# Mean of x squared on 16 columns instead of 512, its norm spread through DRAM on SyncE's queue, and two constant rows loaded through GpSimd's queue

## The chip, the cores and the metric

One core of a Trainium2 chip runs the whole program. The metric is the device time of one execution in microseconds (us); lower is better. TensorE (PE in the profile) multiplies matrices, VectorE (DVE), ScalarE (ACT) and GpSimd (POOL) work on tiles of 128 partitions, and SyncE (SP) issues most of the transfers between memory (DRAM) and the on-chip tiles. ACT and POOL can issue transfers too; each of the three has its own queue, and all of them are carried out by the core's 16 DMA engines.

## The reference

One block of a streaming encoder on 512 positions of 1024 channels. What the change touches is its first step, the root-mean-square norm of the input x and the product of the normed x with `w_in`, and the layer norm of v in the spatial gating unit, with its scale g_v and offset b_v:

```python
def rms_norm(x, g):
    xf = x.astype(jnp.float32)
    y = xf * lax.rsqrt(jnp.mean(xf * xf, axis=-1, keepdims=True) + EPS)
    return (y * g.astype(jnp.float32)).astype(x.dtype)

    hn = rms_norm(h, g_mix_pre[i])
    proj = hn @ w_in[i]
    z_sgu, z_conv, z_pool, z_gate = jnp.split(proj, SPLITS, axis=-1)

def spatial_gating(z, w_s, b_s, g_v, b_v):
    u, v = jnp.split(z, 2, axis=-1)
    v = layer_norm(v, g_v, b_v)
    ...
```

Behind this stand a convolution branch, a pooling branch, three gates, a SwiGLU layer and a gated embedding, which the change leaves as they are.

## The kernel before, in words

Activations lie with channels on partitions: a tile of 128 channels x 512 positions, eight tiles (`KT`) for the 1024 channels. Every operand of a product is split into a high and a low part (`hi`, `lo`, type fp32r), and a product is three matmuls per tile of 128 channels: hi x hi, hi x lo and lo x hi (`mm3`). PE therefore runs through one long row of matmuls of 128x512, each with 128x128 weights.

The start of the program is arranged so that PE need not wait for the norm of x. `first_product` multiplies x, scaled by `g_mix_pre` but not yet normed (tiles `xg`, split by `x_high` on ACT and `x_low` on DVE), with six blocks of weights (`first`, `first_raw`), 18 matmuls for each of the eight channel tiles k, into the six banks `ps_first`. The norm is multiplied in afterwards, when `glu` reads these banks (`sig<-ps_first,x_inv`). While those matmuls run, DVE and ACT work out the norm: the squares of the eight x tiles are added into `x_sums` (128x512), `split_sums` splits that into two halves, two matmuls with a 128x128 matrix of 1/1024 (`channel_mean`) give the mean, the same in all 128 partitions, and `rsqrt`, eight DVE operations of 128x512, gives `x_inv`, 1/rms for every position on every partition. Then eight tiles `hn` are made: DVE multiplies x by gain and `x_inv` (`nrm`), ACT rounds that to the high part, DVE subtracts for the low part. All products behind `ps_first` read `hn`, the first of them `ps_ag`.

The later two norms of the kernel (`h_inv` and `conv_inv`) go another way, which this change uses for x too. `part_sums` transposes the 128x512 sums in blocks of 32x32 and adds along the free axis, which leaves four partial sums per position in a tile of 128x16 (`parts`, split in `part_halves`). `part_mean` adds those with two matmuls of 128x32 weights (`quarters`) on 16 columns. `rsqrt` then runs on 32x16 (`few`). `spread` transposes the result, writes it as one row of 512 numbers to DRAM (`row_home`) and reads that row back into all 128 partitions.

Weights come through `Weights`: SP loads a raw block (128x1024, three buffers), and it is split into `hi` and `lo` (three buffers each) a fixed number of blocks ahead of its product. For the blocks of the first stage from channel tile 5 on, and for the first two blocks `raw` behind them, the split is `split_dma`: ACT writes the high part and its negative, and a transfer on POOL's queue adds the raw block to it in memory (`accum_op`). From then on the split is one cast on ACT and one subtraction on DVE. The `hi` and `lo` of channel tile 7 of the first stage lie in buffers of that same ring, so the third block (`raw`, `hi`, `lo` of `ps_ag`'s third product) can be split only after PE has read them for the last time.

The rows g_v and b_v of the layer norm of v are loaded as two broadcasts of 128x1024 (`g_bc`, `b_bc`) into buffers that the first stage's weights give back; they are used from some 140 us on.

The order of the work is that of the code inside `with order()`; elsewhere a scheduler places it. The part from `x_square` to `hn` is in such a block as far as DVE's and ACT's own instructions go; a split of a weight block, and what `glu` does, are placed among them by the scheduler. An engine works its instructions off in a fixed order, and a transfer is issued when the engine that issues it has got to it and what it waits for has come.

Of the kernel before, what the change touches and what calls it, by code (L numbers as in the profile page):

```python
# [15 lines left out]
P = 128  # L16
T = 512
H = 256
D = 1024
KT = D // P  # L20
NB = T // P
Q = 32
# [71 lines left out]
def hybrid_block(  # L94
# [7 lines left out]
    nc = tc.nc  # L102
# [20 lines left out]
    def slot(tag, name, dt=F32R, shape=(2, T)):  # L123
        return act.tile([P, *shape], dt, tag=tag, name=name, bufs=6 if tag == "tm" else 8)

    def t2(name, n=T):
        return tmp.tile([P, n], F32, tag="t2", name=name)

    def row(name):
        return stat.tile([P, T], F32, tag="row", name=name)  # L130
# [7 lines left out]
    def first_cuts(k):  # L138
        return ((0, 2 * P), (2 * P, N_FIRST)) if k == 0 else ((0, N_FIRST),)
# [14 lines left out]
    def col(name, k):  # L154
        i = VECS.index(name) * KT + k
        return vec[:, i:i + 1]
# [16 lines left out]
    few = [const.tile([Q, Q], F32, name=f"few{i}") for i in range(3)]  # L173
# [15 lines left out]
    def split(hi, lo, src):  # L189
        act_e.copy(hi, src)  # L190
        dve.tensor_tensor(out=lo, in0=src, in1=hi, op=ALU.subtract)
# [52 lines left out]
    def blk(w, k):  # L244
        return w[:, k * P:(k + 1) * P]
# [33 lines left out]
    def rsqrt(y, a, t):  # L279

        dve.tensor_scalar(out=y.bitcast(I32), in0=a.bitcast(I32), scalar1=-0.5,
                          scalar2=RSQRT_SEED, op0=ALU.mult, op1=ALU.add)
        dve.tensor_tensor(out=t, in0=y, in1=y, op=ALU.mult)
        dve.scalar_tensor_tensor(out=t, in0=t, scalar=-RSQRT_C2 * RSQRT_S, in1=a,
                                 op0=ALU.mult, op1=ALU.mult)
        dve.scalar_tensor_tensor(out=y, in0=t, scalar=RSQRT_C1 * RSQRT_S, in1=y,
                                 op0=ALU.add, op1=ALU.mult)
        third_order(y, a, t)
# [12 lines left out]
    def third_order(y, a, t):  # L301

        dve.tensor_tensor(out=t, in0=y, in1=y, op=ALU.mult)
        dve.tensor_tensor(out=t, in0=t, in1=a, op=ALU.mult)
        dve.scalar_tensor_tensor(out=t, in0=t, scalar=-10.0 / 3.0 * RSQRT_S ** 2, in1=t,
                                 op0=ALU.add, op1=ALU.mult)
        dve.scalar_tensor_tensor(out=y, in0=t, scalar=5.0 * RSQRT_S ** 4, in1=y,
                                 op0=ALU.add, op1=ALU.mult)

    def channel_mean(sums, halves=None):  # L310


        ps = psum.tile([P, T], F32, tag="pst", name="ps_stat", bufs=1)
        ps = ps[:, :sums.shape[1]]
        if halves is None:
            pe.matmul(ps, lhsT=mean_mat.bitcast(F32), rhs=sums, start=True, stop=True)
        else:
            for i, half in enumerate(halves):
                pe.matmul(ps, lhsT=mean_mat, rhs=half, start=i == 0, stop=i == 1)
        return ps  # L320

    def part_sums(sums):

        turned, parts = t2("turned"), t2("parts", T // Q)
        dve.transpose(out=turned, in_=sums)
        dve.tensor_reduce(out=parts, in_=turned.rearrange("p (c q) -> p c q", q=Q),
                          axis=mybir.AxisListType.X, op=ALU.add)
        dve.tensor_copy(part_halves[:, 0], parts)
        dve.tensor_tensor(out=part_halves[:, 1], in0=parts, in1=part_halves[:, 0], op=ALU.subtract)

    def part_mean():

        ps = psum.tile([P, T], F32, tag="pst", name="ps_stat", bufs=1)[:Q, :T // Q]
        for i in range(2):
            pe.matmul(ps, lhsT=quarters, rhs=part_halves[:, i], start=i == 0, stop=i == 1)
        return ps

    def spread(y, few, turned):

        dve.transpose(out=turned, in_=few)  # L340
        home = dram.tile([1, T], F32, name="row_home")
        nc.scalar.dma_start(out=home.rearrange("o (c a) -> (o c) a", a=Q), in_=turned[:T // Q])
        nc.scalar.dma_start(out=y, in_=home.broadcast_to([P, T]))

    def spread_inv_rms(y):
        inv, t, turned = few
        rsqrt(inv[:, :T // Q], part_mean(), t[:, :T // Q])
        spread(y, inv, turned)

    def split_sums(sums):  # L350
        halves = [tmp.tile([P, T], F32R, tag="t2", name="sum_half") for _ in range(2)]
        split(*halves, sums)
        return halves
# [87 lines left out]
    x_sums = row("x_sums")  # L441
# [8 lines left out]
    def x_high(k):  # L450
        act_e.activation(out=xg[k][:, 0], in_=x_all[:, k], func=AF.Copy, scale=col("g_mix_pre", k))

    def x_low(k):
        dve.scalar_tensor_tensor(out=xg[k][:, 1], in0=x_all[:, k], scalar=col("g_mix_pre", k),
                                 in1=xg[k][:, 0], op0=ALU.mult, op1=ALU.subtract)

    def w_split(k):
        for c0, c1 in first_cuts(k):
            hi, lo = (w[:, c0:c1] for w in first[k])
            (split_dma if k >= DMA_K else split)(hi, lo, first_raw[k][:, c0:c1])  # L460

    def x_square(k):
        add_square(x_sums, x_all[:, k], k, dve)
# [45 lines left out]
    x_inv = row("x_inv")  # L509
# [3 lines left out]
    def first_product(k, passes, js=range(2 * N_RAW)):  # L513
        for w, a in passes:
            for j in js:
                pe.matmul(banks[j], lhsT=blk(first[k][w], j), rhs=xg[k][:, a],
                          start=k == 0 and w == a == 0, stop=k == KT - 1 and w == 1)


    passes = ((0, 0), (0, 1), (1, 0))  # L520
    with order():
        (c0, c1), cut = first_cuts(0)
        hi, lo = (w[:, c0:c1] for w in first[0])
        dve.tensor_copy(hi, first_raw[0][:, c0:c1])
        x_high(0)
        dve.tensor_tensor(out=lo, in0=first_raw[0][:, c0:c1], in1=hi, op=ALU.subtract)
        x_low(0)
        hi, lo = (w[:, slice(*cut)] for w in first[0])
        split(hi, lo, first_raw[0][:, slice(*cut)])
        first_product(0, passes, range(c1 // P))  # L530
        first_product(0, passes, range(c1 // P, 2 * N_RAW))
        x_square(0)
        x_high(1)
        w_split(1)
        x_low(1)
        x_square(1)
        x_square(2)
        first_product(1, passes)
        x_high(2)
        w_split(2)  # L540
        x_low(2)
        for k in range(3, 6):
            x_square(k)
        first_product(2, passes)
        x_high(3)
        w_split(3)
        for k in range(6, KT):
            x_square(k)
        x_low(3)
        for k in (4, 5):  # L550
            x_high(k)
            w_split(k)
            if k == 4:
                x_halves = split_sums(x_sums)
            x_low(k)
        first_product(3, passes[:2])
        ps_x = channel_mean(x_sums, x_halves)
        first_product(3, passes[2:])
        for k in range(4, KT):
            if k >= 6:  # L560
                x_high(k)
                w_split(k)
        weights.ahead(2)
        weights.split = split
        rsqrt(x_inv, ps_x, t2("rs_t"))
        x_low(6)
        x_low(7)
        low = None
        for i in range(KT):
            t = t2("nrm")  # L570
            dve.scalar_tensor_tensor(out=t, in0=x_all[:, i], scalar=col("g_mix_pre", i),
                                     in1=x_inv, op0=ALU.mult, op1=ALU.mult)
            act_e.copy(hn[i][:, 0], t)
            if low:
                low()
            low = lambda i=i, t=t: dve.tensor_tensor(out=hn[i][:, 1], in0=t, in1=hn[i][:, 0],
                                                     op=ALU.subtract)
        low()
        for k in range(4, KT):
            first_product(k, passes)  # L580
# [59 lines left out]
        dve.bn_stats(out=v_stats[:, b, c, :], in_=v)  # L640

    g_bc = slot("tm", "g_bc", F32, (D,))
    nc.sync.dma_start(out=g_bc, in_=gb_v[0:1, :].broadcast_to([P, D]))
    b_bc = slot("tm", "b_bc", F32, (D,))
    nc.sync.dma_start(out=b_bc, in_=gb_v[1:2, :].broadcast_to([P, D]))
    for _ in natural(v_all, v_gelu, TAPS[1]):
        pass
    mv = const.tile([P, NB, 2], F32, name="v_mv")
# [186 lines left out]
    for k in range(KT):  # L835
        ln_center(k)
    part_sums(var_sum)
    spread_inv_rms(conv_inv)
    for k in range(KT):
        ln_out(k)  # L840
# [74 lines left out]
    with order():  # L915
# [18 lines left out]
        for i in range(N_HALF):  # L934
            n = KT - N_HALF + i
            mean = (lambda: inv_rms(o_sums[:, lo_half], o_inv[:, lo_half],
                                    rsqrt=table_rsqrt)) if i == 0 else None
# [36 lines left out]
        def norm_h(done):  # L974
            if done == STAT_H:
                spread_inv_rms(h_inv)
# [191 lines left out]
```

## Time and profile before

| what | number |
|---|---|
| median of 3 runs | 968.01 us (967.85 to 968.63) |
| the profiled execution's own time | 967.84 us |
| its span | 965.9 us |
| PE busy | 960.6 us, 99% of the span, 4331 matmuls |
| DVE busy | 659.8 us, 68% |
| ACT busy | 354.4 us, 37% |
| POOL busy | 72.1 us, 7% |
| granted clock of PE | 1.0 |

The span is from the first to the last instruction of the profiled execution. Rows of the timeline give the start in us, the duration in us, the engine, the line, the operation, and output <- inputs with shapes; `xN` means that N instructions were merged into the row. All of the work of helper functions carries line 81, so operations are told apart by their tiles. What an engine waited for stands in brackets at the end of a row. `ACTq`, `SPq` mean the issue of a transfer by that engine.

### The profile page before, as it was taken

What the parts mean: (1) busy time and instruction counts of PE and PEld (TensorE: products, weight loads), DVE (VectorE), ACT (ScalarE), POOL (GpSimd) and SP (SyncE); (2) the same over time, 40 slices, a digit from 0 to 9 for tenths busy, and PEclk for the clock granted to TensorE, in tenths of its full rate; (3) what the DMA queues carried; (4) which work ended last, traced back from release to release, by engine and by line L of the source; (5) the groups of instructions that cost most, each with busy time, mean ns of one, the idle gap of its engine ahead of it and who ended that gap; (6) DMA issues with size and microseconds to landing.
All of it is one profiled execution on the core that took longest, in us unless ns stands there. A gap on an engine that the chain in (4) does not pass through costs nothing.

```text
span 965.9 us, 11032 instructions
## 1 busy us (share of the span) xinstructions
PE 960.6 (99%) x4331; PEld 797.1 (83%) x4331; DVE 659.8 (68%) x870; ACT 354.4 (37%) x471; POOL 72.1 (7%) x55
## 2 busy tenths in 40 slices
PE   9999999999999999999999999999999999999998
PEld 6888888888888888888888988888888888888886
DVE  7987899999997799985655786544454432223583
ACT  7622323343124432247435444333232322223451
POOL 1100014001013602220000000000000000000000
PEclk9999999999999999999999999999999999999999
DMA  8832332563323233232336313232323233334321
GB/s 299 196 106 89 110 107 66 172 170 117 108 87 99 86 103 106 88 113 95 109 125 211 101 44 98 89 108 88 110 88 100 94 86 100 96 101 143 111 76 56
DMA packets 36837, 107.45 MB, mean 111 GB/s; under 512 B 4273, under 2 KB 8881, under 8 KB 36785
## 3 DMA queue, kind: packets, MB, share of 16 engines
q1 hardware_dynamic: 35568, 103.95, 33.2%
q0 software_dynamic: 720, 2.23, 1.3%
q10 hardware_dynamic: 496, 0.57, 0.2%
q8 instruction: 34, 0.56, 0.2%
q14 instruction: 19, 0.15, 0.0%
HBM read 100.30 MB, written 4.20 MB: 108 GB/s over the span
## 4 chain that ended last, share of the span: by engine, by line
PE 99%; DVE 0%; issue 0%; DVEq 0%
PE ps_f L81 25%; PE ps_gate L81 14%; PE ps_br L81 14%; PE ps_fo L81 12%; PE ps_nat L81 9%; PE ps_ag L81 6%; PE ps_o L81 5%; PE ps_z L81 5%; PE ps_pg L81 5%; PE ps_first L81 3%; PE ps_pool L81 1%; PE ps_ple L81 1%; PE ps_mix L81 1%; PE ps_warm L81 0%; PE ps_stat L81 0%; DVE pg L81 0%
## 5 line engine op out<-in xcount | busy, mean ns | idle before, releaser
L81 ACT CAST hi<-raw 128x1024 fp32r<-128x1024 f32 (+2 forms) x161 | 165.9, 1032 | 441.2 <-PE ps_br L81 83.9
L81 DVE TENSOR_TENSOR lo<-raw,hi 128x1024 fp32r<-128x1024 f32 (+2 forms) x159 | 210.2, 1323 | 108.5 <-ACT hi L81 108.2
L81 PE MATMUL ps_f<-hg,hi 128*128 128x512 f32 (+1 forms) x604 | 183.4, 385 | 0.0
L81 DVE SCALAR_TENSOR_TENSOR acc<-h_conv,vec,acc 128x511 f32<-128x511 f32 (+17 forms) x240 | 177.1, 742 | 4.5
L81 PEld LDWEIGHTS ps_f<-hg,hi 128*128 128x128 f32 x604 | 112.6, 188 | 22.8
L81 PE MATMUL ps_gate<-hn,hi 128*128 128x512 f32 x384 | 118.7, 389 | 0.0
L81 PE MATMUL ps_f<-hg,lo 128*128 128x512 f32 (+1 forms) x302 | 114.4, 385 | 0.0
L81 PE MATMUL ps_fo<-f,hi 128*128 128x512 f32 x352 | 108.4, 389 | 0.0
L81 PEld LDWEIGHTS ps_gate<-hn,hi 128*128 128x128 f32 x384 | 72.1, 188 | 15.0
L81 PE MATMUL ps_nat<-hi,hn 128*128 128x512 f32 x256 | 78.7, 389 | 0.0
L81 PEld LDWEIGHTS ps_fo<-f,hi 128*128 128x128 f32 x352 | 66.1, 188 | 13.7
L81 PE MATMUL ps_gate<-hn,lo 128*128 128x512 f32 x192 | 74.7, 389 | 0.0
L81 PE MATMUL ps_fo<-f,lo 128*128 128x512 f32 x176 | 68.5, 389 | 0.0
L81 PEld LDWEIGHTS ps_f<-hg,lo 128*128 128x128 f32 x302 | 56.3, 188 | 11.2
L81 PEld LDWEIGHTS ps_nat<-hi,hn 128*128 128x128 f32 x256 | 48.0, 188 | 9.9
L81 DVE TENSOR_TENSOR f<-ps_f,h_inv 128x512 f32<-128x512 f32 x22 | 15.2, 689 | 56.5 <-PE ps_f L81 56.5
L81 PE MATMUL ps_nat<-lo,hn 128*128 128x512 f32 x128 | 49.8, 389 | 0.0
L81 PE MATMUL ps_ag<-hn,hi 128*128 128x512 f32 x160 | 49.2, 389 | 0.0
L81 DVE TENSOR_TENSOR silu<-ps_f,h_inv 128x512 f32<-128x512 f32 x22 | 15.2, 690 | 43.7 <-PE ps_f L81 35.9
L81 PEld LDWEIGHTS ps_gate<-hn,lo 128*128 128x128 f32 x192 | 36.0, 188 | 7.4
L81 PE MATMUL ps_br<-pool,hi 128*128 128x512 f32 x128 | 39.7, 389 | 0.0
L81 PE MATMUL ps_z<-hn,hi 128*128 128x512 f32 x128 | 39.7, 389 | 0.0
(229 smaller groups left out, 1450.0 us busy)
## 6 DMA issues: line engine op xcount, KB each, us to landing
raw<-in_w_mix SPq DMA_DIRECT2D x90, 512.0 KB, 3.3
raw<-in_w_ffn_in SPq DMA_DIRECT2D x44, 512.0 KB, 3.3
raw<-in_w_ffn_out SPq DMA_DIRECT2D x16, 448.0 KB, 3.3
raw<-in_w_ffn_out SPq DMA_DIRECT2D x8, 512.0 KB, 3.5
raw<-in_w_ple_gate SPq DMA_DIRECT2D x8, 512.0 KB, 3.8
x_all<-in_xT SPq DMA_DIRECT2D x8, 256.0 KB, 6.6
home<-corners SPq DMA_DIRECT2D x32, 64.0 KB, 2.6
sgu<-home SPq DMA_DIRECT2D x8, 256.0 KB, 2.7
```

Source lines behind the costliest of these rows:

```text
L81: inst = op(*args, **kw)
```

## The change

Three things are done.

- The mean of x squared is made the narrow way: `part_sums` on DVE in place of `split_sums` (ACT and DVE), `part_mean` in place of `channel_mean`, after all 18 matmuls of channel tile 3 instead of after 12 of them, and `rsqrt` on 32x16.
- The result is spread through DRAM to `x_inv`, by two transfers that wait for one another. `spread` gets a parameter for the queue; for x it is SP's, for the other two norms it stays ACT's.
- `g_bc` and `b_bc` are loaded through POOL's queue.

```diff
-    def spread(y, few, turned):
+    def spread(y, few, turned, queue=nc.scalar):
 
         dve.transpose(out=turned, in_=few)
         home = dram.tile([1, T], F32, name="row_home")
-        nc.scalar.dma_start(out=home.rearrange("o (c a) -> (o c) a", a=Q), in_=turned[:T // Q])
-        nc.scalar.dma_start(out=y, in_=home.broadcast_to([P, T]))
-
-    def spread_inv_rms(y):
+        queue.dma_start(out=home.rearrange("o (c a) -> (o c) a", a=Q), in_=turned[:T // Q])
+        queue.dma_start(out=y, in_=home.broadcast_to([P, T]))
+
+    def spread_inv_rms(y, queue=nc.scalar):
         inv, t, turned = few
         rsqrt(inv[:, :T // Q], part_mean(), t[:, :T // Q])
-        spread(y, inv, turned)
+        spread(y, inv, turned, queue)
...
             if k == 4:
-                x_halves = split_sums(x_sums)
+                part_sums(x_sums)
             x_low(k)
-        first_product(3, passes[:2])
-        ps_x = channel_mean(x_sums, x_halves)
-        first_product(3, passes[2:])
+        first_product(3, passes)
+        spread_inv_rms(x_inv, nc.sync)
...
         weights.split = split
-        rsqrt(x_inv, ps_x, t2("rs_t"))
         x_low(6)
         x_low(7)
...
     g_bc = slot("tm", "g_bc", F32, (D,))
-    nc.sync.dma_start(out=g_bc, in_=gb_v[0:1, :].broadcast_to([P, D]))
+    nc.gpsimd.dma_start(out=g_bc, in_=gb_v[0:1, :].broadcast_to([P, D]))
     b_bc = slot("tm", "b_bc", F32, (D,))
-    nc.sync.dma_start(out=b_bc, in_=gb_v[1:2, :].broadcast_to([P, D]))
+    nc.gpsimd.dma_start(out=b_bc, in_=gb_v[1:2, :].broadcast_to([P, D]))
```

Beyond what the diff says, the scheduler places a few instructions differently. On DVE, at the end of the making of `hn`, where `hn_181` to `hn_184` are the tiles of channels 4 to 7, `lo<-raw,hi` is the third weight block's split and `sig` the first read of `ps_first` by `glu`:

```order
 L81 TENSOR_TENSOR hn_181<-nrm,hn_181 128x512
 L81 SCALAR_TENSOR_TENSOR nrm<-x_all,vec,x_inv 128x512
+L81 TENSOR_TENSOR lo<-raw,hi 128x1024
 L81 TENSOR_TENSOR hn_182<-nrm,hn_182 128x512
 L81 SCALAR_TENSOR_TENSOR nrm<-x_all,vec,x_inv 128x512
+L81 TENSOR_TENSOR sig<-ps_first,x_inv 128x512 x3
 L81 TENSOR_TENSOR hn_183<-nrm,hn_183 128x512
-L81 TENSOR_TENSOR sig<-ps_first,x_inv 128x512 x3
-L81 TENSOR_TENSOR lo<-raw,hi 128x1024
 L81 TENSOR_TENSOR hn_184<-nrm,hn_184 128x512
```

The weight split has moved ahead of the low parts of channel tiles 5, 6 and 7, and the three reads `sig` ahead of that of tile 6. ACT's cast for the same weight block has moved likewise, from ahead of tile 7's cast to ahead of tile 5's.

On POOL, the place where it issues the transfers of the first stage; `few` and `row_home` are not here but on SP:

```order
 L202 DMA lo<-first_raw 128x768
-L202 DMA lo<-raw 128x1024 x2
+L202 DMA lo<-raw 128x1024
+L641 DMA g_bc<-in_gb_v 128x1024
+L202 DMA lo<-raw 128x1024
+L643 DMA b_bc<-in_gb_v 128x1024
 L486 TENSOR_TENSOR conv_sum<-acc_173 128x512
```

`g_bc` now stands between the two transfers that finish the first two weight blocks of `ps_ag`, and `b_bc` behind both. On SP the two transfers of the spread stand where `g_bc` and `b_bc` stood, behind three weight blocks and ahead of all the others:

```order
 L217 DMA raw<-in_w_mix 128x1024
-L643 DMA g_bc<-in_gb_v 128x1024
-L645 DMA b_bc<-in_gb_v 128x1024
+L342 DMA row_home<-few_123 16x32
+L343 DMA x_inv<-row_home 128x512
 L217 DMA raw<-in_w_mix 128x1024 x15
```

SP's row is otherwise the same. On PE the two matmuls of the mean are replaced by the two small ones six matmuls later, and nothing else moves.

## The prediction

> **What bounds the kernel now.** I read the page's busy shares first, then the chain that ended last, then the list of PE's waits, because these three together say whether time saved on another engine can count at all.
>
> ```profile
> PE 960.6 (99%) x4331; PEld 797.1 (83%) x4331; DVE 659.8 (68%) x870; ACT 354.4 (37%) x471; POOL 72.1 (7%) x55
> ```
> ```profile
> PE 99%; DVE 0%; issue 0%; DVEq 0%
> ```
> ```profile
> PE ps_warm L81 <- DVE warm_up L81: 1.3, 1, 1.3
> ```
>
> The first line has PE busy 99% of the span; the second says that the chain which set the end is PE from start to end; the third is the only wait that PE has in the whole run, 1.3 us before its first matmul. So there is no gap to close. The time changes in two ways only: by matmul time added or removed, which counts in full, and by a wait that PE gets anew, which counts in full too, since nothing later on PE has slack to give it back. What DVE, ACT and the queues gain is worth nothing by itself. The question is therefore whether `hn` still comes in time.
>
> PE's timeline gives the dates by which things are needed:
>
> ```profile
> 20.64 0.63 PE L81 MATMUL ps_stat<-sum_half,mean_mat 128*128 128x512 f32 x2
> 21.10 13.80 PE L81 MATMUL ps_first<-xg,first 128*128 128x512 f32 x60
> ...
> 37.46 1.52 PE L81 MATMUL ps_first<-xg,lo 128*128 128x512 f32 x6
> 38.82 0.61 PE L81 MATMUL ps_ag<-hn,hi 128*128 128x512 f32 x2
> ...
> 42.90 0.61 PE L81 MATMUL ps_ag<-hn,hi 128*128 128x512 f32 x2
> 43.35 0.39 PE L81 MATMUL ps_ag<-hn,lo 128*128 128x512 f32 x1
> ```
>
> From 21.10 to 37.46 run 72 matmuls, 0.227 us apart. `ps_ag` begins at 38.82 and takes a channel tile every 0.68 us (six tiles to 42.90), in each a matmul on the high part of `hn` and 0.23 later one on the low part. Tile 6's low part is so used at 43.13, tile 7's at 43.81. DVE's timeline shows when they are made:
>
> ```profile
> 19.87 0.68 DVE L81 TENSOR_TENSOR sum_half<-x_sums,sum_half 128x512 fp32r<-128x512 f32 x1
> 20.47 1.41 DVE L81 SCALAR_TENSOR_TENSOR xg<-x_all,vec,xg 128x512 fp32r<-128x512 f32 x2
> 21.80 0.69 DVE L81 TENSOR_SCALAR x_inv<-ps_stat 128x512 int32<-128x512 int32 x1
> ...
> 28.80 1.41 DVE L81 SCALAR_TENSOR_TENSOR nrm<-x_all,vec,x_inv 128x512 f32<-128x512 f32 x2
> ...
> 35.90 0.74 DVE L81 SCALAR_TENSOR_TENSOR nrm<-x_all,vec,x_inv 128x512 f32<-128x512 f32 x1
> ...
> 37.16 0.74 DVE L81 SCALAR_TENSOR_TENSOR nrm<-x_all,vec,x_inv 128x512 f32<-128x512 f32 x1
> 37.82 0.68 DVE L81 TENSOR_TENSOR hn<-nrm,hn 128x512 fp32r<-128x512 f32 x1
> 38.42 1.88 DVE L81 TENSOR_TENSOR sig<-ps_first,x_inv 128x512 f32<-128x512 f32 x3
> 40.22 1.21 DVE L81 TENSOR_TENSOR lo<-raw,hi 128x1024 fp32r<-128x1024 f32 x1
> 41.35 0.68 DVE L81 TENSOR_TENSOR hn<-nrm,hn 128x512 fp32r<-128x512 f32 x1
> ```
>
> DVE has no pause here. Tile 6's low part ends at 37.82 + 0.68 = 38.50, 4.6 us ahead of its use, tile 7's at 42.03, 1.8 us ahead. That lead is what the change can use up.
>
> **The change, part by part.** *PE's mean.* The two old matmuls hold the row up from 20.64 to 21.10, 0.46 us. What the small ones take is seen at the later norm that has them already:
>
> ```profile
> 435.07 0.39 PE L81 MATMUL ps_gate<-hn,hi 128*128 128x512 f32 x1
> 435.30 0.20 PE L81 MATMUL ps_stat<-part_halves,quarters 128*32 128x16 f32 x2
> ...
> 435.68 0.39 PE L81 MATMUL ps_gate<-hn,lo 128*128 128x512 f32 x1
> ```
>
> Start of hi to start of lo is 0.61 there and 0.45 without (42.90 to 43.35), so the pair costs 0.16 and the change takes 0.30 us off PE. Every date of PE above becomes 0.30 earlier. This is all the gain that there is.
>
> *The sums on DVE.* `part_sums` takes the place of `sum_half` at 19.87:
>
> ```profile
> 429.38 0.71 DVE L81 STREAM_TRANSPOSE turned<-var_sum 128x512 f32<-128x512 f32 x1
> ...
> 431.05 0.18 DVE L81 TENSOR_TENSOR part_halves<-parts,part_halves 128x16 fp32r<-128x16 f32 x1
> ...
> 435.57 0.16 DVE L81 TENSOR_SCALAR few<-ps_stat 32x16 int32<-32x16 int32 x1 [2.29 <-PE ps_stat L81]
> ```
>
> From transpose to the last half are 1.67 + 0.18 = 1.85 us, so the halves are ready at 21.72. PE gets there after six more matmuls of tile 3, 20.64 + 6 x 0.227 = 22.00: no wait, by 0.28 us. The two `xg` follow at about 21.64 and take 1.33 (20.47 to 21.80), so the small `rsqrt` starts at 22.97. ACT is relieved of a cast, DVE of seven eighths of `rsqrt`: nothing on the path, as DVE then only waits.
>
> *The spread.* This is the new link. Both later norms have it:
>
> ```profile
> 437.37 0.33 ACTq L342 DMA_DIRECT2D row_home<-few  x1
> ...
> 438.71 0.34 ACTq L343 DMA_DIRECT2D conv_inv<-row_home  x1
> ```
> ```profile
> 442.70 3.70 DVE L81 TENSOR_TENSOR acc<-acc,conv_inv 128x512 f32<-128x512 f32 x6 [3.83 <-DMA conv_inv<-row_home]
> ```
> ```profile
> 576.89 0.32 ACTq L342 DMA_DIRECT2D row_home<-few  x1
> 581.38 0.33 ACTq L343 DMA_DIRECT2D h_inv<-row_home  x1
> ```
> ```profile
> 584.64 0.69 DVE L81 TENSOR_TENSOR silu<-ps_f,h_inv 128x512 f32<-128x512 f32 x1 [7.78 <-DMA h_inv<-row_home]
> ```
>
> From the start of `rsqrt` to the first issue are 437.37 - 435.57 = 1.80 us, so `row_home` is issued at 24.77. SP's own queue does not hold it, since the last of the blocks ahead of it was issued at 15.19:
>
> ```profile
> 15.19 0.33 SPq L217 DMA_DIRECT2D raw<-in_w_mix  x1
> ```
>
> The write then took 1.34 us for `conv_inv` and 4.49 for `h_inv`, the read 3.99 and 3.26: pairs of 5.33 and 7.75. The load on the DMA engines differed:
>
> ```profile
> 437.00:438.00 1.00, 1.00 (x6) 0.81 (x6) 0.65 (x3) 1.00 (x2) 0.00 (x0) 1.00 0.00 0
> ```
> ```profile
> 576.00:577.00 1.00, 1.00 (x6) 0.83 (x5) 0.72 (x5) 0.00 (x0) 0.00 (x0) 1.00 1.07 131
> ...
> 579.00:580.00 1.00, 1.00 (x7) 0.81 (x6) 0.00 (x0) 0.00 (x0) 0.00 (x0) 1.00 0.00 0
> ```
> ```profile
> 28.00:29.00 1.00, 1.00 (x6) 0.84 (x5) 1.00 (x3) 1.00 (x2) 0.39 (x1) 1.00 1.18 235
> ```
>
> The last two columns are the share of the 16 engines and GB/s: idle at the quick write, full at the slow one, and full (1.18) where x_inv's transfers will fall, because POOL's adding transfers run there. The slow write is the nearer row; but in its last part the engines were idle again (0.00 at 579), so I take 3.8, a little under it. For the read of 256 KB the bounds are 3.26 and what the broadcasts of twice the size took in this very place:
>
> ```profile
> lo<-raw POOLq DMA_DIRECT2D x2, 512.0 KB, 10.0
> ...
> g_bc<-in_gb_v SPq DMA_DIRECT2D x1, 512.0 KB, 5.8
> b_bc<-in_gb_v SPq DMA_DIRECT2D x1, 512.0 KB, 8.9
> ```
>
> `b_bc` stood behind `g_bc` in its queue, so `g_bc`'s 5.8 is the fair upper bound; I take 4.5, between that and the 3.99 of `conv_inv`. `x_inv` then lands at 24.77 + 3.8 + 4.5 = 33.07, and DVE, which started `nrm` at 28.80, stands idle until then. The ends are 1.34 + 3.26 = 4.60 (29.4) and 4.49 + 5.8 = 10.3 (35.1), or 13.4 (38.2) should the read fare as `b_bc` did.
>
> The Trainium skill bears on this choice. Its page "DMA: Bandwidth & Descriptors", section "Queues, rings and completion order", has each engine go round the queues packet by packet, and a completion signal land only after all earlier writes of that engine, of other queues too. By that, `row_home` and `x_inv` each wait behind POOL's transfers, which is what the 4.49 beside a share of 1.07 looks like; it speaks for the upper half of my ends.
>
> *The order on DVE.* From the first `nrm` to the seventh are 7.10 us (28.80 to 35.90) and 0.66 more to the next instruction. There the weight split now stands: 1.13 (40.22 to 41.35), then tile 5's low part 0.60 (37.82 to 38.42), the last `nrm` 0.66, three `sig` 1.80 (38.42 to 40.22), and then tile 6's low part, 0.68 to its end. From the first `nrm` to that end: 7.10 + 0.66 + 4.19 + 0.68 = 12.63 us; before it was 9.70. With `x_inv` at 33.07 tile 6 is ready at 45.70; PE wants it at 43.13 - 0.30 = 42.83. **PE waits 2.87 us.** Tile 7's low part ends 0.60 later and is wanted 0.68 later, so it adds nothing.
>
> Even an early `x_inv` does not bring the wait to nothing, because the weight split cannot start before PE has read the last `lo` of `ps_first`, 37.46 + 1.52 - 0.30 = 38.68; before, it started 1.2 us after that. Then tile 6 is ready at 38.68 + 4.19 + 0.68 = 43.55, and PE waits 0.72. That floor holds for `x_inv` up to 30.9.
>
> *g_bc and b_bc.* SP is rid of two issues that held nobody up. On POOL `g_bc` stands ahead of the transfer that finishes the second block of `ps_ag`:
>
> ```profile
> 29.43 0.86 POOL L202 DMA_DIRECT2D lo<-raw  x1 [1.04 <-ACT lo L81]
> ```
>
> Issued at 29.43 it landed some 10 us later, 39.4; its `lo` is needed when the second product starts, 38.82 + 8 x 0.68 = 44.26, less 0.30 and plus the wait above. `g_bc` adds one issue (0.86 is POOL's for such a transfer) and 512 KB ahead in the queue, while SP's 1 MB that it competed with is gone. I cost it at nothing, as 4.5 us and more lie between; if `g_bc` held POOL's queue longer than that, this block would be PE's next wait.
>
> *Sum*, on the profiled execution's 967.84 (span 965.9): -0.30 + 2.87 = +2.57, so 970.4. The median of the runs is 0.17 above that execution, which makes 970.6.
>
> **The rivals.** One: *the transfers are quick* and the kernel is not slower in a measurable way. No change can be told from this kernel's scatter within 0.2%, 1.94 us; the wait must be 2.24 for that, which is `x_inv` at 32.44, or 7.67 us for the pair of transfers. Under that the verdict is no change; at `conv_inv`'s 5.33 `x_inv` comes at 30.1, the floor decides, and the time is 967.84 - 0.30 + 0.72 = 968.3, 968.4 by the median. For it: one of two pairs seen was so quick, and SP's queue is empty. Against: the engines were idle then and are full here, and the slower pair, 7.75, is above the point already. The skill's page has on its side a fit in the section "Anatomy of one DMA — SWDGE (gpsimd) path", 2.0 us and the bytes at 436 GB/s, which as an estimate gives 2.0 + 2.6 = 4.6 for the pair and so the floor.
>
> Two: *x_inv comes far later*, if POOL's queue keeps the engines as full as at 28. With `b_bc`'s 8.9 behind a write of 4.49, x_inv is at 38.2 and the wait 8.0: 975.7. Against: in that spell `b_bc` also stood behind 512 KB of its own queue.
>
> Three: *g_bc holds the second block back.* If that transfer lands 8.9 us later (one more `b_bc`), at 48.3, PE, which by then wants it at 46.8, waits 1.5 more: 972.1. Against: the queue of SP, which slowed POOL's to 10 us, is nearly empty there.
>
> Four: *nothing but the matmuls changes*, 967.5 by the sum: it needs tile 6 at 42.83, which the floor excludes unless the split's wait for PE is not real. Faster by over 0.2% has no mechanism, as PE gives up 0.30 us.
>
> **How the numbers follow.** Slower by my sum, with the pair between 7.67 and 10.4 us: 0.50. Quick transfers: 0.33, all within 0.2%. Much later x_inv or a late second block, 972 to 976: 0.12. Matmuls alone: 0.05, of which I give 0.02 to faster. So slower 0.62, same 0.36, faster 0.02. The range runs from just under the floor's 968.4 to 973.6, which is above the 35.1 case (wait 4.9, 972.6) and leaves out most of rivals two and four.
>
> **What would show it.** In the profile after, PE's list of waits should have a row `ps_ag` <- DVE `hn` of 2 to 4 us in total, at about 43; DVE an idle time of some 7 us that ends with the landing of `x_inv` at about 33; `ps_stat` at about 22.0 without a wait; and PE's busy time lower by 0.3. A pair of transfers near 5 us, or no `hn` wait, shows the first rival; a wait of PE on `lo` for a transfer shows the third. I would be wrong altogether if PE waits at `ps_stat`, or for work after 50 us.

## The result, and the profile after

The changed kernel takes 975.76 us (median of 5 runs, 975.61 to 977.0) against 968.1 us before (5 runs): a ratio of 1.0081, 95% interval 1.0069 to 1.0092. It is slower, as forecast, but by 7.7 us where 2.6 were forecast, and the time lies above the range, which ended at 973.6. The profiled execution is the 977.0 us one, span 974.9, so 9.0 us over the span before; 1.2 us of the 9.0 is this execution's distance from its median, and the terms below are read against 9.0.

PE's share of the page and its list of waits:

```profile
PE 965.2 (99%) x4331; PEld 799.3 (82%) x4331; DVE 656.7 (67%) x874; ACT 353.8 (36%) x470; POOL 73.2 (8%) x57
```
```profile
PE ps_ag L81 <- DVE hn L81: 4.4, 5, 2.1
PE ps_warm L81 <- DVE warm_up L81: 1.3, 1, 1.3
```

The new wait is where it was expected, `ps_ag` for `hn`, but in five pieces that sum to 4.4 us. PE's busy time, which should have fallen by 0.3, has risen by 4.6: part of the loss doesn't show as waiting at all. Below, the matmuls themselves turn out longer for a while.

The chain behind the wait, on SP, in the list of transfers (issue to landing) and on DVE:

```profile
25.25 0.34 SPq L342 DMA_DIRECT2D row_home<-few  x1
28.47 0.34 SPq L343 DMA_DIRECT2D x_inv<-row_home  x1
```
```profile
lo<-raw POOLq DMA_DIRECT2D x2, 512.0 KB, 8.6
...
g_bc<-in_gb_v POOLq DMA_DIRECT2D x1, 512.0 KB, 9.1
b_bc<-in_gb_v POOLq DMA_DIRECT2D x1, 512.0 KB, 12.2
...
x_inv<-row_home SPq DMA_DIRECT2D x1, 256.0 KB, 8.1
row_home<-few SPq DMA_DIRECT2D x1, 2.0 KB, 3.2
```
```profile
36.60 1.42 DVE L81 SCALAR_TENSOR_TENSOR nrm<-x_all,vec,x_inv 128x512 f32<-128x512 f32 x2 [10.07 <-DMA x_inv<-row_home]
...
44.37 1.21 DVE L81 TENSOR_TENSOR lo<-raw,hi 128x1024 fp32r<-128x1024 f32 x1
45.51 0.68 DVE L81 TENSOR_TENSOR hn<-nrm,hn 128x512 fp32r<-128x512 f32 x1
46.11 0.74 DVE L81 SCALAR_TENSOR_TENSOR nrm<-x_all,vec,x_inv 128x512 f32<-128x512 f32 x1
46.77 1.87 DVE L81 TENSOR_TENSOR sig<-ps_first,x_inv 128x512 f32<-128x512 f32 x3
48.57 1.28 DVE L81 TENSOR_TENSOR hn<-nrm,hn 128x512 fp32r<-128x512 f32 x2
```

The write took 3.2 us and the read 8.1. `x_inv` lands at 36.6, DVE has stood idle for 10.07 us, and the order at the end is the one that the listing of the change showed: split, tile 5's low part, `nrm`, three `sig`, and then the low parts of tiles 6 and 7. PE at that place, and then the granted clock there (the third column from the right of the table by windows, where 1.00 is full speed; the number behind PE's busy share in brackets counts its matmuls):

```profile
39.10 0.62 PE L81 MATMUL ps_ag<-hn,hi 128*128 128x512 f32 x2
...
46.24 0.50 PE L81 MATMUL ps_ag<-hn,hi 128*128 128x512 f32 x1 [1.43 <-DVE hn L81]
...
49.30 0.80 PE L81 MATMUL ps_ag<-hn,hi 128*128 128x512 f32 x1 [2.09 <-DVE hn L81]
...
55.26 0.62 PE L81 MATMUL ps_ag<-hn,hi 128*128 128x512 f32 x2
```
```profile
48.00:49.00 1.00, 0.00 (x0) 0.00 (x0) 1.00 (x3) 0.99 (x2) 0.00 (x0) 0.60 0.20 78
49.00:50.00 1.00, 0.70 (x2) 0.61 (x3) 1.00 (x3) 1.00 (x3) 0.00 (x0) 0.50 0.00 0
...
54.00:55.00 1.00, 1.00 (x3) 0.73 (x3) 1.00 (x2) 0.00 (x0) 0.00 (x0) 0.50 0.08 16
55.00:56.00 1.00, 1.00 (x6) 0.82 (x5) 0.93 (x3) 0.00 (x0) 0.00 (x0) 0.98 0.95 319
```

While PE stood idle its granted clock fell to one half, and it stayed there until 55.0, long after work had come back: three or four matmuls per us instead of six or seven. The 14 matmuls from 49.30 to 55.26 took 5.96 us where 14 x 0.2267 = 3.17 would do (0.2267 is a third of the 0.68 per channel tile): 2.79 us more.

The sum: `ps_ag` starts 0.28 us later than before, at 39.10 against 38.82. From there to tile 6's low part are 10.20 us, where before there were 4.31: 5.89 us of lost time. (The list has 4.4 of it as waits, and the rest is counted as busy: from 41.32 to 42.58, say, three matmuls that are 0.68 us of work take 1.26 us, and the list has only 0.30 of that as a wait.) The half clock adds 2.79. Together 8.96 of the 9.0. After 56 us the distance stays the same: the first `ps_gate` matmul, at 183.0 before, is at 192.0.

### The profile page after: what moved, and what is told of

Same layout as the page of the kernel before. It is cut to its first block, busy times and chain, and to the rows that moved or that the text cites. A ratio compares the mean times of both kernels' runs of the same rounds, so it can differ in the third digit from the quotient of the medians.

```text
span 974.9 us, 11043 instructions
## 1 busy us (share of the span) xinstructions
PE 965.2 (99%) x4331; PEld 799.3 (82%) x4331; DVE 656.7 (67%) x874; ACT 353.8 (36%) x470; POOL 73.2 (8%) x57
## 4 chain that ended last, share of the span: by engine, by line
PE 94%; DVE 2%; DMA 2%; issue 0%; ACT 0%; SPq 0%; DVEq 0%
PE ps_f L81 25%; PE ps_gate L81 13%; PE ps_br L81 13%; PE ps_fo L81 12%; PE ps_nat L81 9%; PE ps_ag L81 5%; PE ps_o L81 5%; PE ps_z L81 4%; PE ps_pg L81 4%; PE ps_pool L81 1%; PE ps_ple L81 1%; DMA x_inv<-row_home 1%; DMA first_all<-in_w_first 1%; PE ps_mix L81 1%; DVE hn L81 0%
## 5 line engine op out<-in xcount | busy, mean ns | idle before, releaser
L81 PE MATMUL ps_ag<-hn,hi 128*128 128x512 f32 x160 | 52.9, 408 | 4.4 <-DVE hn L81 4.4
L81 PEld LDWEIGHTS ps_ag<-hn,hi 128*128 128x128 f32 x160 | 31.3, 196 | 13.4 <-DVE hn L81 6.9
```

The lines of the kernel that those rows point to most:

```text
L81: inst = op(*args, **kw)
```

## The experiments

Three theories were left to separate: that the rows `g_bc` and `b_bc` fill the DMA engines while `x_inv` is read; that the queues matter rather than the load; that POOL's adding transfers alone are to blame. Beside these stood the price of the order on DVE and of the clock. All runs in one table; "read" is `x_inv` from issue to landing, "piece" PE's longest wait for `hn` or what follows, "clock" the lowest value in any window of 1 us from 30 to 65 us.

| kernel | write | read | first `nrm` | piece | clock | median us | ratio (95%) |
|---|---|---|---|---|---|---|---|
| changed | 3.2 | 8.1 | 36.60 | 2.09 | 0.50 | 975.76 | 1.0081 (1.0069 to 1.0092) |
| norm alone | 2.9 | 8.9 | 36.91 | 2.09 | 0.50 | 976.19 | 1.008 (1.0065 to 1.0095) |
| rows alone | - | - | 29.23 | none | 1.00 | 968.41 | 1.0003 (0.9994 to 1.0012) |
| rows late | 3.0 | 4.8 | 32.80 | 2.28 | 0.50 | 971.9 | 1.0036 (1.0023 to 1.0049) |
| 26 fillers | 2.9 | 7.2 | 35.36 | none | 1.00 | 973.58 | 1.0054 (1.0037 to 1.0071) |
| 14 fillers | 3.0 | 7.4 | 35.16 | 1.72 | 1.00 | 972.91 | 1.0048 (1.0033 to 1.0063) |
| no adding | 1.3 | 6.9 | 33.78 | 3.20 | 0.50 | 972.43 | 1.0044 (1.003 to 1.0058) |
| neither | 1.3 | 3.4 | 30.88 | 0.44 | 1.00 | 968.18 | 1.0 (0.999 to 1.0009) |
| order, both engines | 3.0 | 7.2 | 35.26 | 2.75 | 0.50 | 976.92 | 1.0089 (1.0074 to 1.0104) |
| order, DVE alone | 3.6 | 7.6 | 35.63 | 1.00 | 1.00 | 971.58 | 1.0035 (1.0023 to 1.0048) |
| neither, with order | 1.3 | 3.3 | 31.26 | none | 1.00 | 967.57 | 0.9993 (0.9984 to 1.0002) |

**Norm alone.** The changed kernel with the rows back on SP's queue; there they are issued between the write and the read.

```diff
-    nc.gpsimd.dma_start(out=g_bc, in_=gb_v[0:1, :].broadcast_to([P, D]))
+    nc.sync.dma_start(out=g_bc, in_=gb_v[0:1, :].broadcast_to([P, D]))
```
(and `b_bc` likewise)

> The norm part alone: the two rows g_bc and b_bc are loaded on SP again. SP's order then puts them between the write of row_home and the read of x_inv. Theory (the read of x_inv is slow because other transfers fill the 16 DMA engines, and PE's wait follows from it): the read is now behind 1 MB of its own queue and lands later than the 36.6 us of the changed kernel, by 0 to 4 us, since b_bc took 8.9 us at this place before; time 976 to 981. Rival (the rows on POOL's queue are what delays x_inv, and off that queue it is quick): x_inv at 31 to 33, time 968.5 to 971.

```profile
24.96 0.34 SPq L342 DMA_DIRECT2D row_home<-few  x1
25.44 0.37 SPq L641 DMA_DIRECT2D g_bc<-in_gb_v  x1
26.76 0.33 SPq L643 DMA_DIRECT2D b_bc<-in_gb_v  x1
27.95 0.83 SPq L343 DMA_DIRECT2D x_inv<-row_home  x1
```

976.19 us, the read 8.9. The rival is out: off POOL's queue the read is not quick. But in SP's queue the rows also stand ahead of the read, so this run doesn't tell waiting behind them from sharing the engines with them. The third part of the change, the rows' move, neither cost nor saved anything that the intervals can tell.

**Rows alone.** The kernel before, with only the rows moved to POOL's queue.

> The rows alone: the norm of x as before, g_bc and b_bc on POOL's queue. Theory: PE waits for nothing new, 968.1 within 0.1%; the second block of ps_ag lands in time although g_bc stands ahead of it. Rival (POOL's queue holds that block back): a wait of PE at the second product of ps_ag, 969 to 972.

968.41 us, no new wait of PE. Where `x_inv` doesn't come through DRAM, the rows on POOL's queue cost nothing that the interval can tell.

**Rows late.** The changed kernel, with both rows loaded by SP behind the natural v loop, after 100 us.

```diff
     for _ in natural(v_all, v_gelu, TAPS[1]):
         pass
+    nc.sync.dma_start(out=g_bc, in_=gb_v[0:1, :].broadcast_to([P, D]))
+    nc.sync.dma_start(out=b_bc, in_=gb_v[1:2, :].broadcast_to([P, D]))
```

> The changed kernel, with g_bc and b_bc loaded by SP some 60 us later, so that 1 MB less is in flight while x_inv is read; the adding transfers of POOL stay. Theory: x_inv lands 1 to 4 us sooner, at 33 to 35.5, and PE's wait shrinks by as much or more, time 969 to 974. If the adding transfers alone do it, x_inv stays at 36 to 37 and the time at 975 to 976. Rival (a read of a row just written to DRAM takes 8 us whatever else runs): 8 us again, 975 to 976.

```profile
x_inv<-row_home SPq DMA_DIRECT2D x1, 256.0 KB, 4.8
```
```profile
45.51 0.64 PE L81 MATMUL ps_ag<-hn,hi 128*128 128x512 f32 x1 [2.28 <-DVE hn L81]
```
```profile
45.00:46.00 1.00, 0.49 (x2) 0.40 (x3) 1.00 (x3) 0.60 (x2) 0.00 (x0) 0.86 0.11 20
46.00:47.00 1.00, 1.00 (x4) 0.81 (x3) 1.00 (x3) 0.00 (x0) 0.00 (x0) 0.50 0.95 319
...
49.00:50.00 1.00, 1.00 (x6) 0.83 (x5) 1.00 (x2) 0.00 (x0) 0.00 (x0) 0.94 0.00 0
```

Without the rows the read takes 4.8 us and the time falls by 3.9 us to 971.9. This is the load that the prediction had priced: a read of 4.8 where it had put 4.5, `x_inv` at 32.8 where it had put 33.07, a wait of 2.28 where it had put 2.87. It still comes out 1.3 us above 970.6, and the windows show why: a wait of 2.28 us is enough for the clock to fall, just after PE has resumed at 45.51. The mean of 0.86 in window 45 is 0.28 us at one half; with three whole windows and 0.12 us of window 49 that makes 3.4 us at half clock, so 1.7 us lost: 968.07 - 0.30 + 2.28 + 1.7 = 971.75 for the 971.9 measured. The fall isn't certain, though: of the five executions four have a mean granted clock of 0.997 or 0.998 and 971.83 to 972.41 us, and one has 1.000 and 970.33 us.

**26 fillers, 14 fillers.** The changed kernel with matmuls on constant data between the first product and `ps_ag`, whose result nobody reads. They leave the norm's path through DRAM as it is and give PE work meanwhile.

```diff
+        ps = psum.tile([P, T], F32, tag="pst", name="ps_fill", bufs=1)
+        for _ in range(26):
+            pe.matmul(ps, lhsT=warm_up[:, :P], rhs=warm_up, start=True, stop=True)
```

> The changed kernel with 26 extra matmuls of constants (nothing of their result is used) on PE between ps_first and ps_ag, which fill some 5.9 us in which PE would wait. Theory (PE's clock is halved for 6 us because PE had stood idle): the wait is as long but PE is not idle, the clock stays at 1.0, and the 2.8 us that the half clock cost go: 972 to 974. Rival (the half clock comes from something else, or the records show it so only by chance): 975.5 to 977, and the clock falls again.

> The changed kernel with 14 matmuls on constant data put between the first product and ps_ag (their result is not used): 14 of 0.21 us fill 3 us of the 5.9 that PE waits, some 2.9 us of wait remain. It tells what length of wait makes the clock fall. If a remaining wait of about 2 us in one piece still makes it fall, as it did where the rows come late: 974.3 to 975.3. If the sum over a window counts and is now too small: clock 1.0 throughout and 973.2 to 973.8, as with 26 such matmuls.

```profile
47.87 0.50 PE L81 MATMUL ps_ag<-hn,hi 128*128 128x512 f32 x1 [1.72 <-DVE hn L81]
```
```profile
47.00:48.00 1.00, 0.13 (x1) 0.13 (x2) 1.00 (x3) 0.99 (x3) 0.00 (x0) 1.00 0.00 0
48.00:49.00 1.00, 1.00 (x5) 0.82 (x6) 1.00 (x3) 1.00 (x3) 0.00 (x0) 1.00 0.00 0
```

With 26 the time is 973.58, with 14 972.91 (rows of the 14 above): idle work makes the kernel 2.2 and 2.85 us faster by the medians. The profiled executions can be set beside one another with their landings: 977.0 and 972.76 lie 4.24 us apart, of which 36.60 - 35.16 = 1.44 is that `x_inv` landed earlier in the run with 14, and 2.80 is left. With 14 PE still waits 1.72 us in one piece, but the clock stays at 1.00. The 26 are too many: PE gets to `ps_ag` only at 44.5 and no wait is left. So the second part of the loss is the clock, 2.8 us as in the sum above. The two expectations for 14 aren't decided: the clock stayed up, as by the second, and the time came out 0.3 us under its 973.2, but the remaining piece was 1.72 us and not the 2 of the first.

**No adding.** The changed kernel without POOL's adding transfers at the head; DVE splits those blocks, one of them ahead of the small `rsqrt`.

```diff
-DMA_K = 5
+DMA_K = 8
...
-        weights.ahead(2)
         weights.split = split
+        weights.ahead(2)
```

> The changed kernel without POOL's adding transfers at the head: those blocks of the first weights are split by DVE like the others, one of them ahead of the small rsqrt (some 0.95 us later). g_bc and b_bc stay on POOL's queue. DVE makes all low parts of hn before it splits the next block. My theory: x_inv's read took 8.1 us because two things filled the DMA engines, the rows (1 MB) and the adding transfers. With the rows alone it should take 4.8 to 6.5 us (4.8 was what it took beside the adding transfers alone), so x_inv at 33.5 to 35, tile 6's low part 9.7 later at 43.2 to 44.7, a wait of 0.3 to 1.6 us, 968.3 to 970. Rival A: the rows alone are the cause: read 8 us again, x_inv at 37, wait about 3.5 us and a halved clock, 972 to 973.5. Rival B: the adding transfers alone are the cause: read under 4, no wait, 967.7 to 968.2.

```profile
x_inv<-row_home SPq DMA_DIRECT2D x1, 256.0 KB, 6.9
```
```profile
46.48 0.50 PE L81 MATMUL ps_ag<-hn,hi 128*128 128x512 f32 x1 [3.20 <-DVE hn L81]
```

The write takes 1.3 us instead of 3.2, the read still 6.9, the wait is 3.20 in one piece, and the clock falls for 3.4 us: 968.17 - 0.30 + 3.20 + 1.7 = 972.8, measured 972.43 (with 971.31 and 971.84 in the two executions whose mean clock was 1.000, and 974.61 in one with 0.996). It was expected between 968.3 and 970, which failed twice over: the read came out a little above the bound of 6.5, and DVE's order was here not the one expected. The scheduler put `sig` and the split ahead of tiles 6 and 7 once more, so tile 6 came 12.6 us after the first `nrm`, not 9.7. Of the rivals, "the adding transfers alone" is out; "the rows alone" is nearer, with a time inside its 972 to 973.5, but the 8 us of the read are not reached.

**Neither.** Both edits, rows late and no adding.

> The changed kernel with neither on the engines: no adding transfers at the head (as in the run without them), and g_bc and b_bc loaded by SyncE after the natural v loop. My theory: the write and the read run on nearly idle engines and take what they took for conv_inv (1.3 to 1.5 and 3.3 to 4.0 us), x_inv at 30.5 to 31.5, all low parts of hn in time, no wait of PE, full clock; the matmuls' 0.30 us is all that is left, 967.5 to 968.3. Rival: SyncE's queue is slower than ScalarE's by itself, whatever the load: pair of 8 us and more, x_inv at 34 or later, a wait of 0.7 us and more, over 968.8.

```profile
x_inv<-row_home SPq DMA_DIRECT2D x1, 256.0 KB, 3.4
row_home<-few SPq DMA_DIRECT2D x1, 2.0 KB, 1.3
```
```profile
43.57 0.50 PE L81 MATMUL ps_ag<-hn,hi 128*128 128x512 f32 x1 [0.44 <-DVE hn L81]
```

968.18 us, a ratio of 1.0, in the range that was expected, though with a wait of 0.44 us for `hn` where none was. Without this load SP's queue is as quick as ACT's was for `conv_inv`, so the queue is not slow by itself. The engines aren't empty: SP issues the next two weight blocks from 28.52 on, 1.5 us behind the read and in the same queue (in the run without the adding transfers from 28.35 on, in the changed kernel only at 33.00). Side by side, the reads took 3.4 us with neither, 4.8 with the adding transfers, 6.9 with the rows, and with both 7.2 to 8.1 in five profiles with the rows on POOL's queue, against 3.4 + 1.4 + 3.5 = 8.3 if the two delays simply add. The write's delay comes from the adding transfers: 1.3 without them, with the rows or without, and 2.9 to 3.6 with them, 3.0 where the rows came late.

**Order, both engines.** The changed kernel, with DVE and ACT held to an order in which all low parts of `hn` come before `sig` and the third block's split.

```diff
-    for k in range(N_RAW):
-        glu(k, banks[2 * k], banks[2 * k + 1], x_inv)
+    with order():
+        for k in range(N_RAW):
+            glu(k, banks[2 * k], banks[2 * k + 1], x_inv)
...
-            w = weights.get()
+            with order(k == N_RAW):
+                w = weights.get()
```

> The changed kernel with DVE's order written out so that all low parts of hn come before the three sig and before the split of the third block; transfers untouched. My theory: x_inv lands at about 36 as in the changed kernel, tile 6's low part ends 9.7 us later instead of 12.6, so PE waits 2.5 to 3.2 us instead of 5.9, and its clock still falls, though for a shorter time: 971.3 to 973.3. Rival: the order is worth nothing, since the split and sig that now come later make PE wait instead: 975 and more.

```profile
PE ps_ag L81 <- ACT hi L81: 2.7, 1, 2.7
PE ps_warm L81 <- DVE warm_up L81: 1.3, 1, 1.3
PE ps_ag L81 <- DVE lo L81: 0.9, 1, 0.9
PE ps_ag L81 <- DVE hn L81: 0.9, 3, 0.3
```

The rival held: 976.92. The wait for `hn` is down to 0.9, but the edit also put ACT's cast of the third block behind its three sigmoids, each of which waits for DVE, and PE then waits 2.7 + 0.9 us for that block. The price of the order alone stayed open.

**Order, DVE alone.** The same without that fault: DVE does all low parts, then the split, then the three `sig`, and ACT stays with the scheduler.

```diff
+    weights.split = partial(split, kept=True)
+    w_next = weights.get()
+    weights.split = split
+    sigs = [scaled(banks[2 * k + 1], x_inv) for k in range(N_RAW)]
     for k in range(N_RAW):
-        glu(k, banks[2 * k], banks[2 * k + 1], x_inv)
+        glu(k, banks[2 * k], banks[2 * k + 1], x_inv, sigs[k])
```

(`scaled` is `glu`'s first product, and `kept` the split's subtraction, each held in DVE's order.)

> The changed kernel, transfers untouched, with DVE's order alone written out (ScalarE's stays with the scheduler): all low parts of hn, then the split of the third block, then the three sig. It is the run on the order that failed, without its fault there, the casts that were queued behind ScalarE's sigmoids. x_inv lands at 35.2 to 36.6 as in the runs with these transfers. My theory, that the order costs 2.93 us: tile 6's low part ends 9.7 us after the first nrm, at 44.9 to 46.3, so the waits of PE sum to 1.8 to 3.0 us instead of 4.7 to 5.9, in pieces of about 0.3 to 1 us since DVE delivers a tile every 1.27 us and PE uses one in 0.68; 970 to 971.5 if the clock stays up with such short pieces, 971.5 to 972.7 if it falls. Rival: no gain (975 and more), since PE then waits for the split or the product that follows sig.

```profile
PE ps_warm L82 <- DVE warm_up L82: 1.3, 1, 1.3
PE ps_ag L82 <- DVE hn L82: 1.2, 4, 0.3
PE ps_ag L82 <- DVE sig L82: 1.0, 1, 1.0
```

971.58 us, 4.2 less than the changed kernel, with the clock at 1.00 throughout: a little above the 970 to 971.5 that was expected for that case. Tile 6's low part ends 9.72 us after the first `nrm`, as expected. PE reaches it at 45.41, 6.94 us after `ps_ag` began, which is 2.63 more than the 4.31 of before. The waits for `hn` in the list are now pieces of 0.3 us, and a new one of 1.0 stands behind them, which I had not foreseen: the next product's PSUM bank is freed by `sig`, which now comes later. The sum closes: 968.25 - 0.30 + 2.63 + 1.0 = 971.58.

**Neither, with order.** The run with neither, and that order on DVE.

> The kernel with empty DMA engines (no adding transfers at the head, rows loaded after the natural v loop) and the same DVE order written out. x_inv at about 30.4 as there, tile 6's low part at 40.6 instead of 43.4, PE wants it at 42.9: the 0.44 us of wait that was left goes. My theory: all that remains of the change is the matmuls' 0.30 us, 967.4 to 968.0, a ratio of 0.9993 to 1.0000. Rival: the split and sig, now 1.3 us later, make PE wait elsewhere, 968.2 and more.

967.57 us, a ratio of 0.9993 (0.9984 to 1.0002), no wait of PE on `hn` left. The 0.7 us below before agree with the 0.30 us of the matmuls, but the interval includes no change: the version isn't shown to beat the kernel before.

## Why the prediction was right or wrong

**PE's mean, no wait at `ps_stat`: right.** `ps_stat` runs without a wait, at 22.61. From it to the first `ps_first<-xg,hi` are 35.02 - 22.61 = 12.41 us with 54 matmuls between; before there were 34.74 - 20.64 = 14.10 us with 60. Less the six matmuls more, 6 x 0.227 = 1.36, the gain is 0.33 for the 0.30 of the forecast. In the run's time it is too small to show: the last version of the table lies 0.7 us below before, with an interval from 1.5 below to 0.2 above. (A slip without effect is the "seven eighths" of `rsqrt`: the small one takes 1.55 us, 23.47 to 25.02, where the wide one took 5.67, 21.80 to 27.47, so about three quarters are saved.)

**The write, 3.8: high by 0.6.** It took 3.2. The row it was placed near, `h_inv`'s 4.49, was the right kind, a write on full engines; the quick 1.3 appears as soon as the adding transfers are gone.

**The read, 4.5: the first step that failed.** It took 8.1 in the profiled execution and 7.2 to 7.6 in four others with the same transfers. The error lies in one sentence, "I cost it at nothing", on `g_bc` and `b_bc`. I asked only whether the rows would hold the second weight block back, which they don't, and took SP's 1 MB as "gone". It had only moved to POOL's queue: the rows are issued around the read of `x_inv`, at 28.47, and so run beside it:

```profile
27.32 0.85 POOL L641 DMA_DIRECT2D g_bc<-in_gb_v  x1
...
29.20 0.86 POOL L643 DMA_DIRECT2D b_bc<-in_gb_v  x1
```

The bound of 5.8 was taken from `g_bc`, which itself had 512 KB of its kind behind it, not 1 MB in another queue around it. Rows late gives the price: 8.1 - 4.8 = 3.3 us in the profiled execution, 2.4 to 2.8 in the four others, and the 4.8 is what the prediction's 4.5 was an estimate of. The Trainium skill, "DMA: Bandwidth & Descriptors", section "Queues, rings and completion order", has each DMA engine take turns between queues packet by packet; that rows in POOL's queue slow a read in SP's queue from 4.8 to 8.1 agrees with it. The prediction cited this rule for the upper half of its ends, and then took for the read about the middle of 3.26 to 5.8, with an upper end that the measured 8.1 passed by 2.3.

**The order on DVE, 12.63 us: right to 0.07.** 36.60 + 12.63 = 49.23, and PE's matmul on tile 6's low part starts at 49.30. PE's wait follows: wanted at 42.83 plus the 0.58 us by which this execution's head was late, 43.41, so 5.82 against the 5.89 measured. (The head scatters: in the profiles without fillers `ps_ag` begins between 38.47 and 39.33, the latest of them in rows alone, which has the old mean.) The floor of 0.72 was never tested: its reason was that the split must wait for PE until 38.68, and in no profile did DVE come to that split before 40.22. In the run with neither, `nrm` started at 30.88 behind DVE's own work, and 30.88 + 12.63 = 43.51 is 0.54 past PE's 38.66 + 4.31 = 42.97 (the list has 0.44 of it as a wait): the order alone makes it. Rival one's 968.4 is near the 968.18 of that run, so that rival had the right time for another load: its quick pair was seen only without the rows and the adding transfers (1.3 + 3.4 = 4.7), and beside both the pair took 10.1 to 11.3.

**The missing term: the clock.** The sum counted a wait of PE at its length. Here a long wait was followed by a granted clock of one half for 3.4 or 6.8 us, and in the profiled execution that added 2.79 us; all five executions have the same mean clock of 0.996. The profile before left the question open: PE has no wait in it after the first microseconds. The fillers show the price, 2.80 us once the landing of `x_inv` is allowed for. The executions of one kernel show it too, as time goes with the mean granted clock of the execution: in norm alone 974.53 us at 1.000, 975.92 at 0.998, and 976.46 and 977.12 at 0.996. How long PE waited in those that were not profiled is not on record.

**Rival two** (`x_inv` at 38.2, 975.7) named the time that came out. It had the slow read nearly right, 8.9 for 8.1, but its write was 1.3 us too long, so that `x_inv` came 1.6 us too late, and its sum had no clock. That the time agrees is chance. **Rival three** didn't occur: PE waits for no `lo` of the second block. **Rival four**, and faster with it, didn't occur either.

The terms that separate the forecast from the profiled execution, 9.0 - 2.57 = 6.4 us: wait 5.89 - 2.87 = 3.0, clock 2.8, head 0.6. The median is 1.2 us lower; that its read is the shorter one of the other profiles is likely, but only the one execution was profiled.

## What to carry to other kernels

When a value that used to stay on the chip is sent through DRAM, list every transfer in flight in the window of its landing, those that the same change moves included, and price the read beside them: here 3.4, 4.8, 6.9 and 7.2 to 8.1 us for the same 256 KB. When PE, always busy until then, gets its first wait of some 2 us, don't count the wait alone; look at the granted clock in the windows behind it, and if the wait can't be removed, break it up (pieces of 0.3 to 1 us left the clock alone in the run with DVE's order) or fill it with idle matmuls.

## What the runs showed of the hardware

The granted clock of PE fell to 0.50 in or after idle spells and stayed so for 3.4 or 6.8 us, by the windows: 6.8 in the changed kernel (the 0.60 in window 48 makes 0.8 us at one half, six whole windows follow, and 0.04 us of window 55) and in norm alone, 3.4 in rows late, without the adding transfers and with the order on both engines. In the profiled executions a wait of 2.28 us or more in one piece was followed by it each time, and one of 1.72 or less among full work never; but rows late, norm alone and the run without the adding transfers also have executions with a mean clock of 1.000, so the same kernel can escape it; in norm alone it fell already ahead of the 2.09 us wait, after 1.44 us and several of 0.3, so the condition is not the longest piece alone, and where it lies isn't settled. The Trainium skill, "TensorE: Matmul & The Clock Gate", section "Part 1: The HAM clock gate (the "warmup" mystery)", describes windows of about 3.4 us that run freely, half the clock after an idle one and the full clock after a busy one. The lengths of 3.4 and 6.8 agree with that; but the idle window does not: where PE had waited only 2.28 us, no such window can have been idle from end to end, so by that rule one that was idle for at most two thirds was enough.

The 2 KB write to DRAM took 1.3 us without the adding transfers and 2.9 to 3.6 us beside them: a small transfer isn't spared by its size.
